# A 32-byte shift of the activation tiles in SBUF, in a two-layer transformer kernel

## The chip, the core and the metric

The kernel runs on one core of a Trainium2 chip. The metric is the time of one execution on the device, in microseconds (us). A measurement of this kernel is a median over a few executions.

## The reference

Two layers are applied to 256 tokens of width 1024, all in float32. Each layer has three steps, every one ended by a layer norm: a gated feed-forward block, a mixer, and a second feed-forward block.

```python
for l in range(DEPTH):                       # DEPTH = 2
    mod = (silu(c) @ ada_w[l] + ada_b[l]).reshape(bsz, 3, 3, 1, D_MODEL)
    u = modulate(h, mod[:, 0, 0], mod[:, 0, 1])
    y = swiglu_ffn(u, w_gate[l, 0], w_up[l, 0], w_down[l, 0])      # 1024 -> 2816 -> 1024
    h = layer_norm(DN_ALPHA * h + 0.5 * mod[:, 0, 2] * y, ...)
    u = modulate(h, mod[:, 1, 0], mod[:, 1, 1])
    y = hybrid_token_mixer(u, w_in[l], ...)  # convolution + state space + attention branches
    h = layer_norm(DN_ALPHA * h + mod[:, 1, 2] * y, ...)
    ...                                      # the second feed-forward block, as the first
```

The weights are read once each; nearly all of the work is the product of a 128x128 weight block with a 128x256 activation block.

## The kernel before

**Weights.** They are streamed from device memory in units of eight 128x128 blocks. A unit lands in a buffer of the pool `raw` (six buffers). Scalar engine (ACT) writes its rounded copy into a buffer of `whi`, and Vector engine (DVE) writes the remainder `raw - whi` into a buffer of `wlo` (four buffers each), both typed as float32r, which Tensor engine (PE) multiplies in one pass.

**Activations.** They lie transposed, features on the partitions: a tile of the pool `big` (tag `b8`, eleven buffers) holds eight blocks of 128x256, so each block is a row of 1024 bytes in every partition. They are split in the same way: `uh` and `ul` (input of a projection), `hh` and `hl` (hidden layer of the feed-forward block), and so on.

**The main product** is `triple` (lines 557 to 559): three matmuls `whi*xh`, `wlo*xh`, `whi*xl` into one PSUM bank. The weight block is the stationary operand, the activation block the moving one. So PE does, over and over, a weight load of 128 columns and a matmul of 256 columns. The first matmuls after a layer norm come from `early` (with `pair`, L573, and `single`, L582), which starts before the norm is known and carries two more columns: its operand `p` has blocks of 258 columns, 1032 bytes apart. In the first block of weights the same helpers run over `uh` and `ul`.

**Order.** A planner (`Plan.schedule`) lays all instructions out with its own costs when the program is built; it knows tile shapes, not addresses. Between long runs of triples it puts small float32 matmuls: sums over features for the norms (`partial`, `combine`), transposes, attention products.

**Addresses.** Pools follow each other in SBUF in the order in which they are opened: `one`, `raw`, `whi`, `wlo`, `pad`, `big`, `tmp`, `m2`, `m3`, `m8`. A buffer of `raw`, `whi` or `wlo` has 4096 bytes per partition, and all of them begin at 128 modulo 256 bytes. A buffer of `big` has 8448 bytes, a multiple of 256, because `wide8` rounds the largest tile up; so all eleven buffers begin at the same place modulo 256. The pool `pad` holds one tile that nothing reads or writes, and only pushes the pools behind it.

Of the kernel before, what the change touches and what calls it, by code (L numbers as in the profile page):

```python
# [10 lines left out]
F32 = mybir.dt.float32  # L11
# [7 lines left out]
P = 128  # L19
# [74 lines left out]
class Buf:  # L94


    def __init__(self, pool, tag, shape, dt, name, psum):
        self.pool, self.tag, self.shape, self.dt, self.name, self.psum = pool, tag, tuple(shape), dt, name, psum
        self.real = None
        self.live = False  # L100
        self.left = 0
        self.end = 0.0
        self.writes, self.reads = [], []
# [253 lines left out]
class Net(Plan):  # L357
# [6 lines left out]
    def __init__(self, ctx, tc, a):  # L364
        super().__init__()
        self.tc, self.nc, self.a = tc, tc.nc, a
        ctx.enter_context(tc.manual_schedule())
        pool = lambda name, bufs, **k: ctx.enter_context(tc.tile_pool(name=name, bufs=bufs, **k))
        self.pools = {
            "one": pool("one", 1), "raw": pool("raw", self.RAW), "whi": pool("whi", self.WHI), "wlo": pool("wlo", self.WLO),  # L370
            "pad": pool("pad", 1), "b8": pool("big", self.BIG), "t": pool("tmp", self.TMP), "m2": pool("m2", 2), "m3": pool("m3", 3), "m8": pool("m8", 8),
            "mm": pool("ps", 2, space=PSUM), "x": pool("px", 6, space=PSUM)}
        self.slots = {"raw": self.RAW, "whi": self.WHI, "wlo": self.WLO, "b8": self.BIG, "t": self.TMP, "mm": 2, "x": 6}
        self.pools["pad"].tile([P, 48], F32, name="pad", tag="pad")
        self.nunit = a["ws"].shape[0]
        self.tile_no = 0
        self.keyed = None
        self.mod = {}
        self.modbuf = {}
        self.splits = {}  # L380
        self.last = []
# [1302 lines left out]
```

## Time and profile before

| | |
|---|---|
| median of three executions | 1663.49 us (1661.08 to 1667.33) |
| the profiled execution | 1663.87 us |
| its span, first to last instruction | 1662.1 us |
| PE busy with matmuls | 97% of the span |
| DVE busy, ACT busy | 83%, 62% |
| mean granted clock of PE | 0.991 of full speed |

The profiled execution is an ordinary one: it lies 0.4 us above the median. A share of busy time says little about PE here, because a matmul's duration (about 0.28 us) is the time from its start to its modelled end, and the next one starts some 0.115 us after it. What tells PE's speed is how many matmuls start in a stretch of time.

### The profile page before, as it was taken

Reading aid. Unit: us, or ns where it says so; the run is one execution under the profiler, and the core shown is the slowest. Engines: PE = TensorE matmul, PEld = TensorE weight load, DVE = VectorE, ACT = ScalarE, POOL = GpSimd, SP = SyncE. Lnnn points to the kernel's source line nnn. Section 1 sums busy time; section 2 is a strip of 40 time slices with the busy share of each in tenths; the row PEclk is TensorE's granted clock in tenths of the full one; section 3 lists DMA queues with packets and bytes.
Section 4 is the critical chain, followed back from the end, with each engine's and each line's share of the span. In section 5 each row is a group of like instructions: output and inputs, shape, how many; then the busy total and the mean of one; then the engine's idle time right before and its main releaser. Section 6 shows DMA issues by size and latency. Waiting matters only on the chain.

```text
span 1662.1 us, 33662 instructions
## 1 busy us (share of the span) xinstructions
PE 1609.3 (97%) x13294; PEld 1532.9 (92%) x13294; DVE 1384.0 (83%) x2743; ACT 1037.2 (62%) x1951; POOL 8.3 (0%) x64
## 2 busy tenths in 40 slices
PE   6999999899999999999999999998999999999997
PEld 6999989889888988999999999897898899989996
DVE  7899789999999986899677885999999987776655
ACT  4654585889836566644474445858897566574543
POOL 0000000000000000000000000000000000000000
PEclk9999999999999999999999999999999999999998
DMA  9899665332276555889767885643332535657661
GB/s 380 324 349 375 209 210 171 111 118 91 89 270 217 179 171 190 292 334 352 249 235 265 309 317 179 226 155 115 102 107 85 189 130 176 190 180 251 217 198 44
DMA packets 85982, 347.09 MB, mean 209 GB/s; under 512 B 9536, under 2 KB 11840, under 8 KB 76096
## 3 DMA queue, kind: packets, MB, share of 16 engines
q1 hardware_dynamic: 85824, 344.94, 59.5%
q8 instruction: 104, 1.70, 0.4%
q14 instruction: 54, 0.44, 0.1%
HBM read 343.86 MB, written 1.05 MB: 208 GB/s over the span
## 4 chain that ended last, share of the span: by engine, by line
PE 92%; ACT 4%; DVE 2%; DMA 1%; issue 1%; SPq 0%; ACTq 0%
PE mm L557 17%; PE mm L558 17%; PE mm L559 17%; PE a L449 3%; PE g L557 2%; PE a L573 2%; PE g L558 2%; PE g L559 2%; PE xb L557 2%; PE mm L449 2%; PE sb L449 2%; PE xb L559 2%; PE xb L558 2%; PE ob L1040 2%; PE tb L453 1%; PE a L582 1%
## 5 line engine op out<-in xcount | busy, mean ns | idle before, releaser
L461 DVE TENSOR_TENSOR wlo<-raw,whi 128x1024 fp32r<-128x1024 f32 x470 | 573.1, 1221 | 149.1 <-ACT whi L498 147.2
L498 ACT ACTIVATE whi<-raw 128x1024 fp32r<-128x1024 f32 x470 | 496.2, 1058 | 315.4 <-PE mm L559 159.2
L557 PE MATMUL mm<-uh,whi 128*128 128x256 f32 x1392 | 390.2, 280 | 0.9 <-DVE h L461 0.9
L558 PE MATMUL mm<-uh,wlo 128*128 128x256 f32 x1392 | 388.9, 279 | 0.0
L559 PE MATMUL mm<-ul,whi 128*128 128x256 f32 x1392 | 388.9, 279 | 0.0
L557 PEld LDWEIGHTS mm<-uh,whi 128*128 128x128 f32 x1392 | 263.9, 190 | 1.8 <-DVE h L461 1.1
L559 PEld LDWEIGHTS mm<-ul,whi 128*128 128x128 f32 x1392 | 262.7, 189 | 0.0
L558 PEld LDWEIGHTS mm<-uh,wlo 128*128 128x128 f32 x1392 | 261.3, 188 | 0.2
L557 PE MATMUL mm<-hh,whi 128*128 128x256 f32 x704 | 197.3, 280 | 0.0
L558 PE MATMUL mm<-hh,wlo 128*128 128x256 f32 x704 | 196.5, 279 | 0.0
L559 PE MATMUL mm<-hl,whi 128*128 128x256 f32 x704 | 196.5, 279 | 0.0
L480 DVE SCALAR_TENSOR_TENSOR ada<-ada,sc 128x1024 f32<-128x1024 f32 x144 | 173.4, 1220 | 17.0 <-DMA ada<-in_ada 16.9
L557 PEld LDWEIGHTS mm<-hh,whi 128*128 128x128 f32 x704 | 133.0, 189 | 1.3 <-issue 1.2
L559 PEld LDWEIGHTS mm<-hl,whi 128*128 128x128 f32 x704 | 133.0, 189 | 0.0
L558 PEld LDWEIGHTS mm<-hh,wlo 128*128 128x128 f32 x704 | 132.4, 188 | 0.1
L557 PE MATMUL g<-uh,whi 128*128 128x256 f32 x384 | 115.2, 300 | 2.6 <-DVE q L461 2.6
L480 DVE SCALAR_TENSOR_TENSOR ca<-ap,vec,ca 128x256 f32<-128x256 f32 x240 | 114.4, 478 | 0.3
L558 PE MATMUL g<-uh,wlo 128*128 128x256 f32 x384 | 107.2, 279 | 0.0
L559 PE MATMUL g<-ul,whi 128*128 128x256 f32 x384 | 107.2, 279 | 0.0
L480 DVE SCALAR_TENSOR_TENSOR acc<-ap,vec,acc 128x256 f32<-128x256 f32 x224 | 107.0, 478 | 0.1
L498 ACT ACTIVATE sg<-mm 128x256 f32<-128x256 f32 x76 | 29.0, 383 | 109.4 <-PE mm L559 109.1
L557 PE MATMUL xb<-uh,whi 128*128 128x256 f32 x256 | 81.4, 318 | 0.0
(340 smaller groups left out, 3691.6 us busy)
## 6 DMA issues: line engine op xcount, KB each, us to landing
raw<-in_ws SPq DMA_DIRECT2D x498, 512.0 KB, 4.1
ada<-in_ada SPq DMA_DIRECT2D x72, 1024.0 KB, 7.5
w<-in_w SPq DMA_DIRECT2D x4, 1024.0 KB, 9.5
x<-in_x SPq DMA_DIRECT2D x8, 128.0 KB, 11.0
out<-r SPq DMA_DIRECT2D x8, 128.0 KB, 1.9
vec<-in_vec SPq DMA_DIRECT2D x2, 321.0 KB, 4.8
cst<-in_cst SPq DMA_DIRECT2D x1, 524.5 KB, 5.7
cb<-in_c SPq DMA_DIRECT2D x1, 512.0 KB, 3.8
```

What stands on the lines that cost most here:

```text
L449: return self.op("PE", cost, lambda: self.nc.tensor.matmul(real(out), lhsT=real(lhsT), rhs=real(rhs), start=start, stop=stop), [out], [lhs ...
L453: self.op("PE", 0.11, lambda: self.nc.tensor.transpose(real(out), real(in_), real(ident)), [out], [in_, ident], key)
L461: lambda: self.nc.vector.tensor_tensor(real(out), real(a), real(b), op), [out], [a, b], key)
L480: self.nc.vector.scalar_tensor_tensor(real(out), real(a), real(s), real(b), op0, op1, **k)
L498: self.nc.scalar.activation(real(out), real(a), f, **k)
L557: mm(o, lhsT=a, rhs=c, start=start, stop=False)
L558: mm(o, lhsT=b, rhs=c, start=False, stop=False)
L559: mm(o, lhsT=a, rhs=d, start=False, stop=stop)
L573: self.nc.tensor.matmul(o, lhsT=lhsT, rhs=rhs, start=first, stop=False)
L582: self.nc.tensor.matmul(o, lhsT=lhsT, rhs=rhs, start=False, stop=stop)
L1040: self.nc.tensor.matmul(real(out), lhsT=real(lhsT), rhs=real(rhs), start=start, stop=stop)
```

## The change

The tile in the pool `pad` grows from 48 to 56 float32 per partition, from 192 to 224 bytes. Everything behind it, the pools `big`, `tmp`, `m2`, `m3` and `m8`, begins 32 bytes later. The tiles of `big` lie at 96 modulo 256 bytes, where they lay at 64. The pools ahead of it, the weights' among them, stay where they are. No instruction is added, taken out or moved on any engine.

```diff
-        self.pools["pad"].tile([P, 48], F32, name="pad", tag="pad")
+        self.pools["pad"].tile([P, 56], F32, name="pad", tag="pad")
```

## Rows read from the trace of the kernel before

**Rows 1.** The page: busy time; the chain that ended last, by engine.
```profile
PE 1609.3 (97%) x13294; PEld 1532.9 (92%) x13294; DVE 1384.0 (83%) x2743; ACT 1037.2 (62%) x1951; POOL 8.3 (0%) x64
...
PE 92%; ACT 4%; DVE 2%; DMA 1%; issue 1%; SPq 0%; ACTq 0%
```

**Rows 2.** PE by stretches: from:to us, length, busy (matmuls that ran in it), clock.
```profile
20.00:57.00 37.00, 37.00 (x328) 1.00 1.00 394
62.00:172.00 110.00, 110.00 (x936) 1.00 0.93 348
176.00:200.00 24.00, 24.00 (x214) 1.00 0.60 197
...
660.00:803.00 143.00, 143.00 (x1216) 1.00 0.89 329
...
1478.00:1616.00 138.00, 138.00 (x1220) 1.00 0.67 221
```

**Rows 3.** Groups of the whole run: count, busy us, mean ns; DVE first.
```profile
L461 DVE TENSOR_TENSOR wlo<-raw,whi 128x1024 fp32r<-128x1024 f32 x470 | 573.1, 1221 | 149.1 <-ACT whi L498 147.2 <-issue 0.4
...
L558 PE MATMUL mm<-uh,wlo 128*128 128x256 f32 x1392 | 388.9, 279 | 0.0
L558 PE MATMUL mm<-hh,wlo 128*128 128x256 f32 x704 | 196.5, 279 | 0.0
L558 PE MATMUL g<-uh,wlo 128*128 128x256 f32 x384 | 107.2, 279 | 0.0
L558 PE MATMUL xb<-uh,wlo 128*128 128x256 f32 x256 | 71.5, 279 | 0.0
```

**Rows 4.** The same groups from 700 to 740 us, then from 1500 to 1540 us.
```profile
L558 PE MATMUL mm<-uh,wlo 128*128 128x256 f32 x114 | 32.0, 281 | 0.0
...
L558 PE MATMUL mm<-uh,wlo 128*128 128x256 f32 x119 | 32.8, 276 | 0.0
```

**Rows 5.** Timeline of PE: start us, duration us, what; at two stretches' beginnings.
```profile
659.28 0.47 PE L557 MATMUL mm<-uh,whi 128*128 128x256 f32 x1
659.59 0.28 PE L558 MATMUL mm<-uh,wlo 128*128 128x256 f32 x1
...
1477.04 0.47 PE L557 MATMUL mm<-uh,whi 128*128 128x256 f32 x1
1477.35 0.28 PE L558 MATMUL mm<-uh,wlo 128*128 128x256 f32 x1
```

**Rows 6.** Timeline of PE in `early`: block 1 of `p`, then block 4.
```profile
204.66 0.29 PE L573 MATMUL a<-p,whi 128*128 128x258 f32 x1
...
205.03 0.28 PE L573 MATMUL a<-p,whi 128*128 128x258 f32 x1
...
207.92 0.28 PE L573 MATMUL a<-p,whi 128*128 128x258 f32 x1
...
208.40 0.28 PE L573 MATMUL a<-p,wlo 128*128 128x258 f32 x1
...
209.40 0.28 PE L573 MATMUL a<-p,whi 128*128 128x258 f32 x1
...
209.87 0.28 PE L573 MATMUL a<-p,wlo 128*128 128x258 f32 x1
```

**Rows 7.** DVE, all instructions of two groups: duration ns min/median/max.
```profile
L480 DVE SCALAR_TENSOR_TENSOR ca<-ap,vec,ca x240: 464/478/488, 237.8 to 1357.4; 128x256 f32<-128x256 f32 x120
L461 DVE TENSOR_TENSOR ca<-ca,acc x16: 414/418/424, 266.3 to 1358.1; 128x256 f32<-128x256 f32 x16
```

**Rows 8.** The page: DMA issues, KB each, us to landing; who waits for `ada`.
```profile
ada<-in_ada SPq DMA_DIRECT2D x72, 1024.0 KB, 7.5
...
vec<-in_vec SPq DMA_DIRECT2D x2, 321.0 KB, 4.8
cst<-in_cst SPq DMA_DIRECT2D x1, 524.5 KB, 5.7
...
  DMA ada<-in_ada: 16.9, 12
```

## The prediction

> **What bounds the kernel now.** I read the page first. PE is busy for 97% of the span and makes up 92% of the chain that ended last [rows 1]. So a nanosecond added to or taken from each matmul shows in the time almost whole, and the other engines matter only where PE waits for them.
>
> The second view is PE by stretches, because a busy share can't show at what pace a busy PE works. I took stretches in which PE does nothing but triples. In 143 us from 660 us there are 1216 matmuls, in 138 us from 1478 us there are 1220 [rows 2]. A stretch also counts the two or three matmuls that were under way at its start (each lasts 0.28 us and the next one starts at less than half of that), so 2.4 come off: 143/1213.6 = 117.8 ns from start to start in the one, 138/1217.6 = 113.3 ns in the other. **The same instruction has two paces, 4.5 ns or 4% apart**, at the same granted clock of 1.00 (2.4 GHz). The other stretches fall on one or the other: 110/933.6 = 117.8, 24/211.6 = 113.4, 37/325.6 = 113.6 [rows 2].
>
> The third view is the matmul's own duration, in which the pace shows as well: 281 ns in a slow stretch, 276 ns in a quick one [rows 4]. That gives the mix over the run. The four largest groups of line 558 hold 388.9 + 196.5 + 107.2 + 71.5 = 764.1 us in 2736 matmuls, 279.3 ns each [rows 3]; (279.3 - 276)/5 = 0.66, so about two thirds run slow and a third quick. How many they are follows from the weights: 470 units are split [rows 3], each has 8 blocks, each block is used in three matmuls, 11,280 in all; without those in which the weights are the moving operand, about 11,000. To these a change in PE's reading of SBUF applies.
>
> **The change part by part.** Nothing is added or removed, and the order on each engine is the same. What remains is the address.
>
> *PE's weight loads* read `whi` and `wlo`, which don't move. Cost nothing.
>
> *PE's moving operand* moves from 64 to 96 modulo 256 bytes, the only place where a small price counts 11,000 times. What does the trace show of addresses? First, the address alone doesn't choose the pace. The stretch from 20 to 57 us and that from 62 us are the same projection from the same tiles `uh` and `ul`, quick in the first and slow from the start of the second [rows 2]. The stretch from 660 us and the one from 1478 us each follow the same native float32 matmuls of `early` and begin alike: a first triple matmul, the next 0.31 us later [rows 5]; one is slow and one is quick. A stretch keeps its pace for up to 1200 matmuls, whatever ACT, DVE and the DMA do beside it, so the pace looks like a phase between weight load and moving stream that is set when PE starts again after a break. Second, the address isn't without effect. In `early` the blocks of `p` are 1032 bytes apart, so block k begins at 64 + 8k modulo 256, with weights placed as ever. Block 1 (at 72) takes (205.03 - 204.66)/3 = 123 ns per matmul; block 4, which begins at 96, just where the change puts everything, takes (208.40 - 207.92)/4 = 120 and (209.87 - 209.40)/4 = 118 ns [rows 6], 119 on the mean. Two columns more than 256 account for 0.8 ns (2 at 2.4 GHz), so 96 reads as about 118, the slow pace, and 72 as 122.5.
>
> So the ends are these. Upper end: every matmul as dear as at 72. The mix now is 0.34 x 113.3 + 0.66 x 117.8 = 116.3 ns; 11,000 x 6.2 ns = +68 us. Lower end: every matmul quick, 0.66 x 11,000 x 4.5 ns = -33 us; nothing in the trace runs below 113.3. Between them lies "the quick pace is gone", 0.34 x 11,000 x 4.5 = +17 us. The nearest row is that of block 4 itself, and it shows a pace that the kernel has today at 64; but `early` has 258 columns and breaks up any steady phase, so it can't show whether the quick pace survives. I take no change, because both paces live at one address today and the break ahead of a stretch picks between them.
>
> The Trainium skill, "TensorE: Matmul & The Clock Gate", Step-by-step, says that the array's two operands have read ports of their own and loading weights takes nothing from the running matmul; by that no address could matter and the change would cost 0. Block 1 against block 4 of `p` speaks against its full form, since only the moving operand's address differs there. The same page (Back-to-back issue gap) gives N/2.4 + 2.5 ns, 109.2 ns for 256 columns, a single pace below both of those here. The sum above uses neither.
>
> *DVE and ACT* read and write shifted tiles. The convolution on DVE reads its input from starts 8 bytes apart (every second tap goes to `ca`, 15 starts), and the 240 instructions take 464 to 488 ns, median 478 [rows 7]: a spread of some 2% either way over all offsets. DVE is busy for 83% [rows 1] beside PE, and would have to lose far more before PE waited. Taken as nothing; without that cover it would be at most 2% of DVE's share.
>
> *DMA* into `big` (`ada`, `x`, the compression weights) lands 32 bytes later; the weight units don't. DVE waits for `ada`, and PE through it, 12 times, 16.9 us in all [rows 8]. The only loads of before that land at 32 modulo 64 bytes are small: `vec`, 321 KB in 4.8 us or 67 KB/us, against `cst` at 128 modulo 256, 524.5 KB in 5.7 us or 92 KB/us [rows 8]. Were that the address, an `ada` load would take 7.5 x 92/67 = 10.3 us, and the 12 waits 34 us more; below, nothing. But `vec` has shorter rows and lands amid other loads, so I take 0.
>
> **The sum** is 1663.9 us for the profiled execution (0.4 above the median of the runs), plus 0: 1664 us.
>
> **The rivals.**
> 1. *The quick pace is gone.* With the moving operand 32 bytes further from the weights' residue, the phase that runs at 113.3 ns no longer holds. For it: block 4 at 96 shows the slow pace only. Against it: at 64 the same `early` shows no steady quick pace either. It decides when the long stretch from 1478 us reads 281 ns: 1664 + 17 = 1681 us.
> 2. *A third, dearer pace*, as at 72: 119 to 122.5 ns, 2.7 to 6.2 ns above today's mean, 1694 to 1732 us. Against it: 96 is a multiple of 16 as 64 is, and block 4 is 4 ns cheaper than block 1.
> 3. *The slow pace becomes rare* (the other side). If the shift separates the two reads better, the stretches from 62 and 660 us read 276 ns; each long one that turns gives 1216 x 4.5 = 5.5 us, two of them pass 0.5%, all of them give 1664 - 33 = 1631 us. For it: two thirds have room to turn, and only a third to lose. Against it: nothing at 96 reads 113 steadily.
> 4. *The loads slow down* by up to 34 us; a small chance, within rival 2's.
>
> **How the numbers follow.** Half a per cent (8.3 us) is about what a measurement can tell here. Forecast (both paces, one long stretch more or less in either): 0.40. Quick pace gone: 0.25. A dearer pace, or slower loads: 0.10. Slow pace rarer: 0.25, of which 0.08 for all or nearly all of it. So faster 0.25, same 0.40, slower 0.35. The range leaves out the dearer paces and the last part of rival 3: from 1640 to 1690 us. The forecast's own range is 1656 to 1672.
>
> **What would show it.** The stretches of triples should still fall on 113.3 or 117.8 ns, 276 or 281 ns of duration, in about the same mix. A single duration in all stretches settles rival 1 or 3; a new one, rival 2. `early`'s block 0 now begins at 96, block 4 at 128, and block 1 at 104: block 1 should fall below 123 ns if it is the address that costs. DVE's and ACT's means should stay within 1%, and `ada` should land in about 7.5 us. What would make the forecast wrong is that the phase depends on the distance between the operands' addresses, so that the break ahead of a stretch no longer decides.

## The result, and the profile after

The changed kernel takes 1684.95 us, median of four executions (1684.71 to 1687.21); the kernel before takes 1665.05 us (1661.08 to 1667.33) in as many. The ratio of the runs on record is 1.0144, 95% interval 1.0116 to 1.0172, and the quotient of the two medians is 1.0120: **slower by 1.2 to 1.4%**, a small change but one clear of noise. The profiled span grew from 1662.1 to 1683.0 us, by 20.9 us, at the same mean clock of 0.991. The forecast of 1664 us, "no change", was wrong; the range of 1640 to 1690 us held the time, and rival 1, the quick pace gone and 1681 us, came nearest.

The page of the changed kernel: busy time, then the chain by engine, as in [rows 1].

```profile
PE 1632.5 (97%) x13294; PEld 1557.0 (93%) x13294; DVE 1385.3 (82%) x2743; ACT 1037.6 (62%) x1951; POOL 8.3 (0%) x64
...
PE 93%; ACT 4%; DVE 2%; DMA 0%; issue 0%; SPq 0%; ACTq 0%
```

PE is busy 23 us longer; DVE and ACT, which read and write shifted tiles too, are within 1.3 us of before. So the time is on PE. Its stretches, columns as in [rows 2], all inside runs of triples but for the first, where `pair` and `single` run over `uh` and `ul`:

```profile
20.00:57.00 37.00, 37.00 (x315) 1.00 1.00 394
64.00:168.00 104.00, 104.00 (x882) 1.00 0.93 345
179.00:203.00 24.00, 24.00 (x205) 1.00 0.62 190
680.00:790.00 110.00, 110.00 (x932) 1.00 0.88 318
875.00:975.00 100.00, 100.00 (x847) 1.00 0.84 295
1515.00:1600.00 85.00, 85.00 (x720) 1.00 0.65 223
```

Read as in the prediction, with 2.4 matmuls taken off each count: 104/879.6 = 118.2, 110/929.6 = 118.3, 100/844.6 = 118.4, 85/717.6 = 118.4 ns, and the two short ones, where one matmul more or less is half a per cent, 118.4 and 118.5. **All stretches now have one pace.** Before there were two, 113.3 and 117.8 ns [rows 2]. The clock column says 1.00 in all of them, before and after, so the throttle has no part in it.

The groups of the whole run, as in [rows 3]:

```profile
L461 DVE TENSOR_TENSOR wlo<-raw,whi 128x1024 fp32r<-128x1024 f32 x470 | 573.6, 1223 | 157.1 <-ACT whi L498 155.5 <-issue 0.3
...
L558 PE MATMUL mm<-uh,wlo 128*128 128x256 f32 x1392 | 391.6, 281 | 0.0
...
L558 PE MATMUL mm<-hh,wlo 128*128 128x256 f32 x704 | 198.1, 281 | 0.0
...
L480 DVE SCALAR_TENSOR_TENSOR ca<-ap,vec,ca 128x256 f32<-128x256 f32 x240 | 114.8, 480 | 0.3
...
L558 PE MATMUL g<-uh,wlo 128*128 128x256 f32 x384 | 108.0, 281 | 0.0
...
L558 PE MATMUL xb<-uh,wlo 128*128 128x256 f32 x256 | 71.9, 281 | 0.0
```

The matmul's mean is 281 ns in each group, where a mixture gave 279; `wlo`, none of whose tiles moved, takes 1223 ns for 1221; the convolution's instruction, whose `ca` moved, takes 480 on the mean, near the old median of 478 [rows 7].

A bookkeeping from the start times in the two traces says whether that is all. Take every pair of neighbouring matmuls of `triple`, and of `pair` and `single` over `uh` and `ul`, that start less than 135 ns apart. Before there are 10,295 such intervals, 1193.8 us in all, 115.96 ns each; after 10,299, 1218.6 us, 118.32 ns each. That is +24.8 us. All else between the starts of PE's first and last matmul went from 443.0 to 439.2 us, -3.8. The sum is +21.0 us; the span grew by 20.9.

### The profile page after: what moved, and what is told of

Read it like the earlier page. It is cut to its first block, busy times and chain, and to the rows that moved or that the text cites. A ratio compares the mean times of both kernels' runs of the same rounds, so it can differ in the third digit from the quotient of the medians.

```text
span 1683.0 us, 33662 instructions
## 1 busy us (share of the span) xinstructions
PE 1632.5 (97%) x13294; PEld 1557.0 (93%) x13294; DVE 1385.3 (82%) x2743; ACT 1037.6 (62%) x1951; POOL 8.3 (0%) x64
## 4 chain that ended last, share of the span: by engine, by line
PE 93%; ACT 4%; DVE 2%; DMA 0%; issue 0%; SPq 0%; ACTq 0%
PE mm L557 18%; PE mm L558 17%; PE mm L559 17%; PE mm L449 3%; PE a L449 3%; PE g L557 2%; PE a L573 2%; PE g L558 2%; PE g L559 2%; PE xb L557 2%; PE sb L449 2%; PE xb L559 2%; PE xb L558 2%; PE ob L1040 2%; PE tb L453 1%; PE a L582 1%
## 5 line engine op out<-in xcount | busy, mean ns | idle before, releaser
L461 DVE TENSOR_TENSOR wlo<-raw,whi 128x1024 fp32r<-128x1024 f32 x470 | 573.6, 1223 | 157.1 <-ACT whi L498 155.5
L480 DVE SCALAR_TENSOR_TENSOR ada<-ada,sc 128x1024 f32<-128x1024 f32 x144 | 173.6, 1221 | 14.3 <-DMA ada<-in_ada 14.3
```

Of the source, the lines that this page charges most:

```text
L461: lambda: self.nc.vector.tensor_tensor(real(out), real(a), real(b), op), [out], [a, b], key)
L480: self.nc.vector.scalar_tensor_tensor(real(out), real(a), real(s), real(b), op0, op1, **k)
```

## The experiments

Call M the place of the activation tiles modulo 256 bytes and W that of the weights' buffers. Before: M = 64, W = 128, M - W = -64. After: M = 96, W = 128, -32. The theories, by the letters used in the expectations:

- **D**: the distance M - W decides which paces exist. It is what the prediction named as the thing that would make it wrong. D128 and D256 are two forms of it (the distance counts modulo 128 or 256).
- **O** (rival): the moving operand's own place decides, modulo 64 or finer, whatever the weights do.
- **T** (rival): the smaller pools behind `big` (`tmp`, `m2`, `m3`, `m8`), which also moved, decide.

The paces below are means of start to start over the 18 runs of at least 100 such matmuls in each trace; every run lies within 0.15 ns of a pace given. A window row shows each in the way used above: length / (count - 2.4). The kernels were measured in three groups, each on one chip with the kernel before beside it; before's own median is given, since it differed from group to group. The ratios are those on record, with their 95% intervals; they differ from the quotients of the medians by up to 0.0024.

**What has to move for the loss.**

`shift_all`: the weights move by 32 bytes as well.

```diff
+        self.pools["pad0"].tile([P, 8], F32, ...)   # new pool, ahead of raw
         self.pools["pad"].tile([P, 48], F32, name="pad", tag="pad")
```

> The weights' pools and the activation pools all begin 32 bytes later: weights at 160, activations at 96 modulo 256, 64 bytes apart as before. Theory D (the distance between the moving operand and the weights decides): two paces again, 113.3 and 117.8 ns, some 1664 us. Theory O (the moving operand's own place modulo 64 decides): 118.3 ns in every stretch, some 1685 us. Theory T (the smaller pools behind the large one decide): 118.3 ns too.

Measured: 1664.86 us against 1662.09, ratio 1.0012 [0.9989, 1.0035]. PE by stretches:

```profile
680.00:790.00 110.00, 110.00 (x973) 1.00 0.91 338
875.00:975.00 100.00, 100.00 (x851) 1.00 0.84 306
```

110/970.6 = 113.3 and 100/848.6 = 117.8 ns: both old paces are back, with the activations at 96 as in the changed kernel. O falls: the place 96 in itself costs nothing.

`shift_weights`: the weights move by 32 bytes, the activations stay at 64; distance -96.

```diff
+        self.pools["pad0"].tile([P, 8], F32, ...)   # new pool, ahead of raw
-        self.pools["pad"].tile([P, 48], F32, name="pad", tag="pad")
+        self.pools["pad"].tile([P, 40], F32, name="pad", tag="pad")
```

> Only the weights' pools begin 32 bytes later (160 modulo 256); the activations stay at 64, 96 bytes below the weights modulo 256 instead of 64. Theory D: neither 113.3 nor 117.8 ns, a pace of its own as with the change, near 118.3 ns and 1685 us. Theory O and theory T: the two paces of before, some 1664 us.

Measured: 1687.37 us, ratio 1.0140 [1.0109, 1.0171].

```profile
680.00:790.00 110.00, 110.00 (x929) 1.00 0.87 315
875.00:975.00 100.00, 100.00 (x854) 1.00 0.84 300
```

118.7 and 117.4 ns (means over the long runs: 118.67 and 117.33). Nothing of `big` has moved, and the loss is as large as the change's: the span grew by 21.2 us where the change's grew by 20.9. The prediction gave PE's weight loads "cost nothing" because they don't move; what counts is where they lie relative to the other operand.

`shift_tail`: only the pools behind `big` move by 32 bytes.

```diff
+        self.pools["pad2"].tile([P, 8], F32, ...)   # new pool, between big and tmp
```

> The large pool stays at 64 modulo 256, only the smaller pools behind it (temporaries, attention tiles) begin 32 bytes later. Theory T: 118.3 ns in every stretch of triples and some 1685 us. Theories D and O: the two paces of before, 1664 us within 8.

Measured: 1661.51 us, ratio 0.9986 [0.9964, 1.0009].

```profile
64.00:168.00 104.00, 104.00 (x920) 1.00 0.95 359
680.00:790.00 110.00, 110.00 (x936) 1.00 0.88 326
```

113.3 and 117.8 ns. T falls.

**Is the pace each matmul's own, or the triple's?** `lo_96`: only `ul` and `hl` are used from 32 bytes into their buffers.

```diff
     def big8(self, name, dt=F32, shape=(P, KT, T)):
-        return self.buf(self.pools["b8"], "b8", shape, dt, name)
+        off = 8 if name in ("ul", "hl") else 0
+        v = self.buf(self.pools["b8"], "b8", (P, 2112), dt, name)[:, off:off + n]   # n elements of shape
+        ...
```

> Only the low parts `ul` and `hl` are moved by 32 bytes, to 96; `uh` and `hh` stay at 64, so two matmuls of a triple keep the distance -64 and the third has -32. If each matmul pays for its own distance: the mean of the triple is one third at 118.33 and two thirds at 113.33 or 117.78 ns, so 115.0 or 118.0 ns, and the time is about a third of the way, near 1671 us. If a triple has one pace for all three and one broken distance is enough to lose the quick one: no stretch below 117 ns, and 1678 us or more.

Measured: 1685.78 us against 1664.30, ratio 1.0133 [1.0105, 1.0160]. The kernel holds its own control, because the mixer's output products use other low parts (`yal`, `ybl`, `mgl`), which weren't moved. Groups of PE, first from 620 to 640 us, then from 690 to 760 us (`triple` stands at L566 to L568 here):

```profile
L566 PE MATMUL mm<-mgh,whi 128*128 128x256 f32 x35 | 9.7, 276 | 0.0
L567 PE MATMUL mm<-mgh,wlo 128*128 128x256 f32 x35 | 9.7, 276 | 0.0
L568 PE MATMUL mm<-mgl,whi 128*128 128x256 f32 x35 | 9.7, 276 | 0.0
...
L568 PE MATMUL mm<-ul,whi 128*128 128x256 f32 x197 | 55.9, 284 | 0.0
L567 PE MATMUL mm<-uh,wlo 128*128 128x256 f32 x197 | 55.6, 282 | 0.0
L566 PE MATMUL mm<-uh,whi 128*128 128x256 f32 x197 | 54.9, 279 | 0.0
```

In the first stretch the matmul takes 276 ns, the quick duration; its pace is 113.4 ns. In the second the pace is 118.88 ns, dearer than a third of 118.33 and two thirds of either old pace, and dearer than with all three matmuls at -32. So a matmul does not pay for its own distance alone: one displaced operand in three costs the whole triple its quick pace. By the start times from 690 to 760 us the next matmul starts 122.1 ns after that of `ul`, and 115.4 and 119.2 ns after those of `uh`: the displaced one is the dearest, but the other two have neither of their old paces either. Here the moving operands also lie apart from each other, which no other kernel has; what part that plays was not separated.

**Does anything further away than 256 bytes matter?** `by_256`: the pool `pad` holds 112 floats, 256 bytes more.

> The pool `pad` holds 112 floats: all tiles of `big` and behind lie 256 bytes later, at the same place modulo 256 as before. D and O alike: 113.33 and 117.78 ns, each stretch on one of them, not necessarily the same stretches as in the profile of before; the time lies where runs of before lie, 1651 to 1669 us (ratio 0.994 to 1.006). If absolute addresses mattered beyond 256 bytes, another pace would show.

Measured: 1663.17 us (1653.82 to 1674.18, ten executions) against 1664.30, ratio 1.0000 [0.9976, 1.0025].

```profile
64.00:168.00 104.00, 104.00 (x920) 1.00 0.94 356
680.00:790.00 110.00, 110.00 (x973) 1.00 0.91 340
875.00:975.00 100.00, 100.00 (x851) 1.00 0.85 310
1515.00:1600.00 85.00, 85.00 (x753) 1.00 0.65 215
```

The two old paces and no other. But the stretches from 64 and from 680 us, slow in the profile of before (62:172 and 660:803 in [rows 2]), are quick here: which pace a stretch gets is not fixed by the program's instructions and their order, which are the same.

**The distance, step by step.** Seven more kernels set M and leave W at 128. The edit is the size of `pad` alone (32, 64, 72 or 80 floats for M = 0, 128, 160, 192); for M = 72 and 80 every tile of `big` is used from 8 or 16 bytes into its buffer, as in `lo_96` but for all names, and for 48 `pad` has 40 floats besides. The expectations:

> The large pool begins 64 bytes later than before, at 128 modulo 256, where the weights are too: a multiple of 64 again, distance 0. Theory O: the two paces of before, some 1664 us. Theory D: one pace of its own, 117.8 ns or dearer, since both reads then start in the same place modulo 256: 1680 us or more.

> The activations lie at 192 modulo 256, 64 bytes above the weights' 128 instead of 64 below. Theory D128 (only the distance modulo 128 counts): the two paces of before, 113.3 and 117.8 ns, some 1662 us. Theory D256 (the distance modulo 256 counts): another set of paces, with a time outside 1662 by over 0.5%.

> The activations lie at 0 modulo 256, 128 bytes from the weights. Theory D128: distance 0 modulo 128, so 120.0 ns in every stretch, as at 128, and some 1700 us. Theory D256: the farthest place from the weights, cheaper than 120 ns, 1690 us or less.

> The pool `pad` holds 72 floats: activations at 160, weights at 128, distance +32 modulo 256. D128 (the distance counts modulo 128): +32 is the same as -96, so the paces of the shifted weights' run, 117.3 and 118.7 ns, in every stretch of triples, and about 1687 us (ratio 1.013 to 1.017). D256 (it counts modulo 256): a pace not seen yet. O (the moving operand's own place modulo 64 decides): 160 is 32 modulo 64 as 96 is, so 118.33 ns alone, as after the change, and about 1685 us; the paces tell the two apart, the time does not.

> The buffers stay where they were, but every tile of the large pool is a view that starts 16 bytes into its buffer: activations at 80 modulo 256, 48 below the weights, half way to the change. If the distance acts in steps of 16 bytes: one pace or a set of its own, between 113.3 and 118.3 ns, 1640 to 1685 us. If it acts in steps of 32 or 64 bytes: the paces of before, 1662 us.

> Activations at 48 modulo 256, 80 below the weights: 16 bytes to the other side (the large pool begins 32 bytes earlier, its tiles start 16 bytes into their buffers). Steps of 16 bytes: a pace or a set of its own, 1640 to 1685 us. Steps of 32 or 64: as before, 1662 us, or as at a distance of 96, 117.3 and 118.7 ns and 1685 us.

> Every tile of `big` is used from 8 bytes into its buffer: activations at 72, distance -56, all else as before. The prediction's upper bound, from block 1 of `p` (123 ns): 11,000 matmuls by 6 ns, 1663 + 66 = 1729 us. D with every broken distance in the band seen so far (117 to 120 ns): 1680 to 1705 us, with a new pace that is none of those. O with steps of 16 bytes or less: slower than before as well. If 8 bytes make no difference: 113.33 and 117.78 ns and 1655 to 1668 us.

Measured, with the kernels above; "mean" is that over the 10,295 to 10,321 intervals of the bookkeeping, and the last column is 1662.1 + 10,300 x (mean - 115.96 ns), the span if nothing but the pace had changed:

| kernel | M - W | paces, ns | mean, ns | median, us (ratio, interval) | span, us | span by the pace |
|---|---|---|---|---|---|---|
| before | -64 | 113.33, 117.78 | 115.96 | 1665.05 | 1662.1 | |
| `shift_tail` | -64 | 113.33, 117.78 | 115.54 | 1661.51 (0.9986, 0.9964 to 1.0009) | 1655.7 | 1657.8 |
| `shift_all` | -64 | 113.33, 117.78 | 116.31 | 1664.86 (1.0012, 0.9989 to 1.0035) | 1662.9 | 1665.7 |
| `by_256` | -64 | 113.33, 117.78 | 115.02 | 1663.17 (1.0000, 0.9976 to 1.0025) | 1652.0 | 1652.4 |
| `at_192` | +64 | 113.33, 117.78 | 117.36 | 1676.50 (1.0105, 1.0063 to 1.0147) | 1672.7 | 1676.5 |
| `at_160` | +32 | 116.67, 117.78 | 117.07 | 1673.51 (1.0053, 1.0028 to 1.0078) | 1672.2 | 1673.5 |
| after | -32 | 118.33 | 118.32 | 1684.95 (1.0144, 1.0116 to 1.0172) | 1683.0 | 1686.4 |
| `shift_weights` | -96 | 117.33, 118.67 | 118.17 | 1687.37 (1.0140, 1.0109 to 1.0171) | 1683.3 | 1684.9 |
| `at_0` | -128 | 118.67, 120.00 | 118.76 | 1689.72 (1.0186, 1.0143 to 1.0229) | 1688.6 | 1690.9 |
| `at_80` | -48 | 116.67, 119.17 | 118.97 | 1692.05 (1.0193, 1.0147 to 1.0239) | 1690.2 | 1693.1 |
| `at_48` | -80 | 119.26 | 119.23 | 1696.32 (1.0224, 1.0173 to 1.0275) | 1694.4 | 1695.8 |
| `at_128` | 0 | 120.00 | 119.85 | 1700.58 (1.0218, 1.0192 to 1.0244) | 1698.4 | 1702.2 |
| `at_72` | -56 | 120.00, 121.67 | 120.55 | 1708.33 (1.0257, 1.0222 to 1.0292) | 1707.8 | 1709.4 |

Before's median was 1662.09 us beside `shift_all`, `shift_weights`, `shift_tail` and `at_128`; 1656.61 beside `at_192`, `at_0`, `at_80` and `at_48`; 1664.30 beside the rest.

Of seven of these traces, the windows that tell the paces. `at_192`: 110/933.6 = 117.8, 24/211.6 = 113.4 ns.

```profile
680.00:790.00 110.00, 110.00 (x936) 1.00 0.88 322
811.00:835.00 24.00, 24.00 (x214) 1.00 0.64 208
```

`at_160`: 117.8, then 100/856.6 = 116.7 ns.

```profile
680.00:790.00 110.00, 110.00 (x936) 1.00 0.88 323
875.00:975.00 100.00, 100.00 (x859) 1.00 0.83 294
```

`at_128`: 110/916.6 = 120.0 ns.

```profile
680.00:790.00 110.00, 110.00 (x919) 1.00 0.87 317
```

`at_72`: 120.0, then 100/821.6 = 121.7 ns.

```profile
680.00:790.00 110.00, 110.00 (x919) 1.00 0.87 319
875.00:975.00 100.00, 100.00 (x824) 1.00 0.82 291
```

`at_0`: 26/216.6 = 120.0, then 110/926.6 = 118.7 ns.

```profile
610.00:636.00 26.00, 26.00 (x219) 1.00 0.58 185
680.00:790.00 110.00, 110.00 (x929) 1.00 0.87 313
```

`at_80`: 24/205.6 = 116.7, then 110/922.6 = 119.2 ns.

```profile
179.00:203.00 24.00, 24.00 (x208) 1.00 0.65 196
680.00:790.00 110.00, 110.00 (x925) 1.00 0.87 312
```

`at_48`: 104/872.6 = 119.2 ns.

```profile
64.00:168.00 104.00, 104.00 (x875) 1.00 0.93 343
```

What follows. First, the spans of the twelve other kernels come out of the pace alone within 4 us, where they reach up to 46 us above before's, so the pace is nearly the whole effect. Second, steps of 8 and 16 bytes count; their prices had been put too low, since `at_80` and `at_48` lie above the 1685 us of their expectations and `at_72` above the 1705 us of D. Third, D128 does not hold: +64 has the two paces of -64, but +32 has not those of -96, nor -128 the single one of 0. Fourth, `at_192` missed its expectation of about 1662 us under D128 though it has the right paces: in its profile only three of the 18 long runs, 250 to 267 matmuls each, are quick, and its four executions, 1674.51 to 1677.65 us, all lie above the seven of before beside them. The distance settles which paces exist, and how often the quick one is taken is a second matter.

No distance gave a stretch below 113.33 ns, and no kernel beats the one before.

## Why the prediction was wrong

*The range held, and that says nothing for the forecast.* It had been drawn wide enough to take in rival 1 as well. The forecast's own range, 1656 to 1672 us, was missed, and so was its mechanism: the trace after shows one pace where both were to stay.

*The measuring of PE's pace was right.* Two paces of 113.3 and 117.8 ns exist at -64 in four kernels. The sizes were a little off: of the about 11,000 matmuls (11,088 in the trace) only 10,295 stand in a steady stream, and the quick share is (117.78 - 115.96)/4.45 = 0.41 where the rounded durations gave 0.34. The stretch from 20 to 57 us, which the prediction set beside the one from 62 us, is not one of triples but of `pair` and `single`, in another order; `by_256`, quick from 64 us where before is slow, bears its point out without that.

*"The sum is 1663.9 us for the profiled execution (0.4 above the median of the runs), plus 0" failed, and the step behind it is "I take no change, because both paces live at one address today and the break ahead of a stretch picks between them."* The pick does vary from break to break (`by_256`, `shift_all` and `shift_tail` got other picks from the same instructions). But it is made among the paces that the distance between the operands offers, and at -32 there is one, 118.33 ns. The reasoning took the moving operand's address as the variable and the weights' as fixed. The sentence that would have corrected it stands at the prediction's end.

*The term, mis-sized.* Instead of 0 it is 10,295 x (117.78 - 115.96) = +18.7 us for the quick pace lost, 10,299 x (118.33 - 117.78) = +5.7 us for a slow pace that became slower, and -3.8 us elsewhere: +20.6 against the span's 20.9. Rival 1 had the first term, as 17 us; rival 2's "third, dearer pace" supplied the second. Rival 1's reason had the direction wrong: 96 is nearer to the weights' 128 than 64 is, not further from it.

*The bounds.* The upper end, every matmul at block 1's 122.5 ns and 1664 + 68 us, was too far: with all tiles at 72 `at_72` ran at 120.0 and 121.7 ns and 2.6% over before. `early`, with 258 columns and its pauses, could give neither that size nor the pace at 96. The sign of block 1 was right. The timeline of PE in `early` after the change, for the matmuls that answer to [rows 6]:

```profile
207.00 0.28 PE L573 MATMUL a<-p,whi 128*128 128x258 f32 x1
...
207.35 0.28 PE L573 MATMUL a<-p,whi 128*128 128x258 f32 x1
...
210.22 0.28 PE L573 MATMUL a<-p,whi 128*128 128x258 f32 x1
...
210.69 0.28 PE L573 MATMUL a<-p,wlo 128*128 128x258 f32 x1
...
211.70 0.29 PE L573 MATMUL a<-p,whi 128*128 128x258 f32 x1
...
212.19 0.28 PE L573 MATMUL a<-p,wlo 128*128 128x258 f32 x1
```

Block 1, now at 104, reads 0.35/3 = 117 ns where it read 123; block 4, now at 128, reads 118 and 122 ns where it read 120 and 118. Such a reading is thin: it has three or four intervals, rounded to 10 ns, those of block 1 stand directly behind a pause, and every third matmul in it takes `pl` of the block before (`early` lets its `single` follow four pairs later), so more than one address differs between the two blocks. Over all intervals under 135 ns in the two passes of `early` that use `p` and `pl`, block 1 goes from 122.5 to 118.1 ns (18 intervals in each trace) and block 4 from 118.1 to 120.1 (16). The sign stands.

*The rule that spoke for 0.* The measured change is +20.9 us of span at an unchanged order of instructions. The Trainium skill, "TensorE: Matmul & The Clock Gate", Step-by-step, gives the two operands ports of their own, so that a weight load takes nothing from the running matmul. By that, as the prediction read it, the change would have cost 0; the measurement decides against that here, though no view shows how the two reads meet. The formula N/2.4 + 2.5 ns of the Trainium skill, same page, Back-to-back issue gap, is there the gap of an isolated matmul, not the pace of a stream with a weight load for each. All paces here lie above its 109.2 ns, and the sum did not use it.

*DVE, ACT and DMA: right.* The largest group of DVE whose tiles moved, before and then after:

```profile
L480 DVE SCALAR_TENSOR_TENSOR ada<-ada,sc 128x1024 f32<-128x1024 f32 x144 | 173.4, 1220 | 17.0 <-DMA ada<-in_ada 16.9
...
L480 DVE SCALAR_TENSOR_TENSOR ada<-ada,sc 128x1024 f32<-128x1024 f32 x144 | 173.6, 1221 | 14.3 <-DMA ada<-in_ada 14.3
```

The convolution's instruction, 480 for 478 ns, is within 0.5% (above). The loads, by the page and the view of waits:

```profile
ada<-in_ada SPq DMA_DIRECT2D x72, 1024.0 KB, 7.3
...
DVE ada L480 <- DMA ada<-in_ada: 14.3, 11, 6.6
```

7.3 us for 7.5 and 14.3 us of waiting for 16.9 [rows 8]: rival 4 has nothing. Rival 3, the slow pace rare, fails too: nothing at -32 is quick.

*What stays open.* Why these distances give these paces was only described, not found: no view shows the reads themselves. That the distance alone decides was tested by moving both operands once, at -64; for the other distances only one operand was moved, so a part played by the operands' own places is not excluded there. What picks the pace at the start of a stretch is open too, and so is whether the quick pace can be had everywhere, which would take 10,295 x (115.96 - 113.33) = 27 us off before's span. The distances +96 and +16 and the place M = 32 were not run.

## What to carry to other kernels

Where PE bounds a kernel with a weight load for every matmul, as in this one (float32r, 256 columns a matmul), take its pace from counts in pure stretches, and look at where the moving operand lies relative to the weights, modulo 256 bytes: here that alone was worth up to 2.6%, at identical instructions. A pool that grows by some bytes ahead of another can therefore be a change to PE's pace, and a comparison of two versions should keep the two operands' places the same or it measures them too. If a stretch shows two paces, ask of an address change which paces it leaves to choose from, before asking which is chosen.

## What was not expected of the hardware

- One distance offers several steady paces (113.33 or 117.78 ns; 116.67 or 119.17; 120.00 or 121.67), kept for up to 1234 matmuls. With the clock at 1.00 (2.4 GHz) 113.33 ns are 272 cycles and 120.00 are 288. Single intervals repeat a pattern: 113, 113, 114 ns in the quick runs; 119, 125, 116 in runs at 120.00 and 120, 127, 123, 117 in those at 121.67, both at -56.
- Which pace each stretch gets makes most of the kernel's spread: the four profiles at -64 span 1652.0 to 1662.9 us, and their mix of the two paces alone gives 1652.4 to 1665.7. Ten executions of `by_256` cover 20 us and ten of `shift_all` 16, while four of the changed kernel, with one pace, cover 2.5 and four of `at_128` 2.2.
- One operand in three at another distance was dearer (118.88 ns) than all three (118.33 ns).
